# One broadcast product of 512 columns in the place of four of 128, its diagonals in one tile

## Chip, cores and metric

One Trainium2 chip (trn2), and one of its cores. The metric is the device time of one execution in microseconds (us). Times of instructions come from one profiled execution of the kernel.

## What is computed

A hybrid encoder layer runs over a prompt of 512 tokens and a sample of 1024 tokens with the same weights (width 1024, f32). It is RMSNorm, one combined input projection, differential attention with four heads beside a gated linear recurrence (RG-LRU), one output projection, RMSNorm, a SwiGLU feed-forward part and a last RMSNorm:

```python
def rmsnorm(x, g):
    xf = x.astype(jnp.float32)
    y = xf * lax.rsqrt(jnp.mean(xf * xf, axis=-1, keepdims=True) + NORM_EPS)
    return (y * g.astype(jnp.float32)).astype(x.dtype)
...
    h = rmsnorm(x, norm_mix)
    proj = h @ w_in
...
    o = diff_attention(q, k, v, lam)
    o = rmsnorm(o, subln_g) * (1.0 - lam_init)
...
    x = x + jnp.concatenate([o.astype(x.dtype), y_lru], axis=-1) @ w_out
    h2 = rmsnorm(x, norm_ffn)
    x = x + (jax.nn.silu(h2 @ w_gate) * (h2 @ w_up)) @ w_down
```

The change concerns the step that turns 1/rms, one number for each token, into a tile that can be multiplied with activations. It serves the norms over the width and the norm of each attention head's output.

## The kernel before

**Layout.** Activations lie feature by token: 128 features on the partitions, 512 tokens (a block) along the free axis. Block 0 is the prompt, blocks 1 and 2 are the sample. Products in full precision are three products of rounded halves each (`mm3`, L213 to L215: activation high and weight high, activation low and weight high, activation high and weight low). A weight's halves are made by ScalarE (`wh`, L200) and VectorE (`wl`, L201), an activation's by L326 and L327.

**Spreading 1/rms.** In this layout a token's sum of squares is a sum over partitions. `inv_rms_cols` (L274) makes it with one product for each 128 tokens, which leaves tokens on the partitions (`ss`, L279), and `rsqrt_cols` (L244) takes 1/sqrt by small VectorE steps (L248 to L253). `bcast_cols` (L256) brings the tokens back to the free axis and copies them to all partitions: it multiplies the identity by a column of 1/rms (`dg`, L261, a 128x128 diagonal matrix, VectorE), and a product with a matrix of ones (L262, TensorE) fills 128 columns of the PSUM bank `bc`. It does this for four groups of 128 tokens (two in the last stage). Each `dg` comes from the pool `small`, with 2 buffers of its own.

**Who calls it.** 22 calls: `load_block` (L297) once for each block, whose `bc` ScalarE copies to the row tile `rms` (L339); `attention` (L478), once for each prompt head and twice for each sample head, whose `bc` scales the head's output `ot` (L607, VectorE); the norm ahead of the feed-forward part; and the last norms (`finish`, L1086).

**The ring "mh".** Tiles of 128x512 f32 that live shortly are handed out by a ring, always in the order in which the program is written; a new one waits until the one that stood so many places before it is no longer used. In the first phase (input projections, recurrence, prompt attention) the ring has 4 buffers (L835), later it has 10 (`M3`, L902). In the first phase it serves the squares of `load_block` (`sqa`, `sq`), the evictions of the projection (`ev`, L375, VectorE multiplies a finished product by `rms`, and L376 stores it by DMA) and the reloads of `out_load` (`ir`, L617).

**Order of the work.** The program is written as generators that are interleaved by a table of shares (`advance`): the projection of the sample is the main stream in the first phase, and prompt attention, the recurrence and the prompt's output projection run as side streams between its products. The scheduler then sets the order on each engine; a row stays in that order on the chip. The projection (`proj`, L355) accumulates in 3 PSUM banks (`mm`, L834). Products of the projection are named `pm`, the gates of the recurrence `pr`, scores `sc`, their transposes `ptw` and `pt`, and the weighted values `pv`.

Of the kernel before, what the change touches and what calls it, by code (L numbers as in the profile page):

```python
# [16 lines left out]
ALU = mybir.AluOpType  # L17
# [3 lines left out]
P = 128  # L21
# [11 lines left out]
HALF = (P, BLK)  # L33
# [48 lines left out]
def build(tc, io, es):  # L82
    nc = tc.nc
    V, A, T = nc.vector, nc.scalar, nc.tensor
# [8 lines left out]
    rings = {}  # L93
# [7 lines left out]
    def small(n, name, bufs=2):  # L101
        return smp.tile([P, n], F32, name=name, tag=name, bufs=bufs)
# [8 lines left out]
    def bank(name, tag):  # L111
        return banks[tag].tile([P, BLK], F32, name=name, tag=tag)
# [13 lines left out]
    ident = cp.tile([P, P], F32, name="ident")  # L126
    nc.scalar.dma_start(ident, io["ident"])
    onesq = cp.tile([P, P], F32, name="onesq")
# [127 lines left out]
    def bcast_cols(tag, r, c0, who="m", n=4):  # L256

        bc = bank("bc", tag)
        for i in range(n):
            dg = small(P, "dg")  # L260
            V.tensor_scalar(dg, ident, r[:, c0 + i:c0 + i + 1], None, ALU.mult)  # L261
            T.matmul(bc[:, i * P:(i + 1) * P], lhsT=onesq, rhs=dg, start=True, stop=True)  # L262
        return bc[:, 0:n * P]

    def rms_rows(tag, x):
# [18 lines left out]
    def inv_rms(tag, acc, n=4):  # L284

        return bcast_cols(tag, inv_rms_cols(tag, acc, n), 0, n=n)
# [11 lines left out]
    def load_block(b, other=None, xring="raw"):  # L298
# [36 lines left out]
        if b:  # L335
            yield YL
        bc = bcast_cols("lru", r, 0)
        rows[b] = rings["rows"](HALF, f"rms{b}")
        A.copy(rows[b], bc)  # L339
# [143 lines left out]
    def attention(s, done, vo):  # L483
# [3 lines left out]
        for hd in range(NH):  # L487
# [116 lines left out]
            for g in range(n // BLK):  # L604
                w = slice(g * BLK, (g + 1) * BLK)
                bc = bcast_cols("pv", r, 4 * g, "a")
                V.scalar_tensor_tensor(ot[:, w], ot[:, w], subg, bc, ALU.mult, ALU.mult)  # L607
                nc.scalar.dma_start(cat[s][hd][:, w], ot[:, w])
                yield 1.5
# [217 lines left out]
    n = (B1 + B2 + 3 + GRP) // 2  # L827
# [49 lines left out]
    bc = inv_rms("pv", sums)  # L877
# [350 lines left out]
```

## Time and profile before

| what | value |
|---|---|
| median of 3 runs | 1773.88 us (1773.84 to 1776.88) |
| the profiled execution | 1773.56 us |
| its span in the trace | 1771.7 us |
| mean granted clock of TensorE, share of 2.4 GHz | 0.993 |
| TensorE busy | 1733.3 us (98%) |
| VectorE busy | 1316.5 us (74%) |
| ScalarE busy | 829.2 us (47%) |
| products of L262 | 168 passes, 26.8 us to 1764.6 us |

The profiled execution is 0.3 us under the median, and its span 1.9 us under its own time. PE is TensorE, DVE VectorE, ACT ScalarE. The busy time of a group of products counts each from its start to its modelled end, and products overlap: one of 512 columns has a length of about 0.4 us, but the next starts 0.23 us after it.

### The profile page before, as it was taken

What the parts mean: (1) busy time and instruction counts of PE and PEld (TensorE: products, weight loads), DVE (VectorE), ACT (ScalarE), POOL (GpSimd) and SP (SyncE); (2) the same over time, 40 slices, a digit from 0 to 9 for tenths busy, and PEclk for the clock granted to TensorE, in tenths of its full rate; (3) what the DMA queues carried; (4) which work ended last, traced back from release to release, by engine and by line L of the source; (5) the groups of instructions that cost most, each with busy time, mean ns of one, the idle gap of its engine ahead of it and who ended that gap; (6) DMA issues with size and microseconds to landing.
All of it is one profiled execution on the core that took longest, in us unless ns stands there. A gap on an engine that the chain in (4) does not pass through costs nothing.

```text
span 1771.7 us, 22720 instructions
## 1 busy us (share of the span) xinstructions
PE 1733.3 (98%) x8316; PEld 1432.2 (81%) x8316; DVE 1316.5 (74%) x2291; ACT 829.2 (47%) x1327; POOL 1.6 (0%) x6
## 2 busy tenths in 40 slices
PE   8999999999999999999999989999999999999997
PEld 7777787777878888888878768888888888888897
DVE  6789878777578777777453797777777777977784
ACT  6568556664355554545242452333233334445451
POOL 0000000000000000000000000000000000000000
PEclk9999999999999999999999999999999999999999
DMA  8533424153373322222364743222233229743261
GB/s 294 193 113 102 152 84 137 60 172 137 115 232 112 105 83 96 77 84 78 125 215 132 258 161 114 89 102 101 98 111 125 89 78 337 256 125 97 95 201 54
DMA packets 105023, 238.77 MB, mean 135 GB/s; under 512 B 12240, under 2 KB 21200, under 8 KB 104912
## 3 DMA queue, kind: packets, MB, share of 16 engines
q1 hardware_dynamic: 76608, 185.04, 32.8%
q10 hardware_dynamic: 28304, 52.28, 7.7%
q8 instruction: 65, 1.06, 0.2%
q14 instruction: 46, 0.38, 0.1%
HBM read 180.00 MB, written 57.28 MB: 134 GB/s over the span
## 4 chain that ended last, share of the span: by engine, by line
PE 84%; DVE 6%; DMA 4%; ACT 3%; issue 1%; SPq 0%; DVEq 0%; ACTq 0%
PE pm L213 5%; PE pm L214 5%; PE pm L215 4%; PE gu L213 4%; PE gu L215 4%; PE gu L214 4%; PE acc L215 4%; PE acc L213 4%; PE acc L214 4%; PE y L213 3%; PE y L214 3%; PE y L215 3%; PE z L214 2%; PE z L213 2%; PE z L215 2%; PE x L213 2%
## 5 line engine op out<-in xcount | busy, mean ns | idle before, releaser
L213 PE MATMUL pm<-xh,wh 128*128 128x512 f32 x480 | 190.5, 397 | 5.6 <-ACT wh L200 3.3
L214 PE MATMUL pm<-xl,wh 128*128 128x512 f32 x480 | 189.7, 395 | 0.8 <-DVE xl L327 0.8
L215 PE MATMUL pm<-xh,wl 128*128 128x512 f32 x480 | 189.4, 395 | 0.0
L200 ACT CAST wh<-wr 128x1024 fp32r<-128x1024 f32 x100 | 104.9, 1049 | 149.9 <-PE gu L214 61.3
L213 PE MATMUL gu<-yh,wh 128*128 128x512 f32 x352 | 142.0, 403 | 0.9 <-DVE ev L375 0.9
L213 PE MATMUL acc<-hp,ws 128*128 128x512 f32 (+1 forms) x396 | 140.9, 356 | 0.0
L215 PE MATMUL acc<-hp,ws 128*128 128x512 f32 (+1 forms) x396 | 140.5, 355 | 0.0
L214 PE MATMUL acc<-hp,ws 128*128 128x512 f32 (+1 forms) x396 | 140.2, 354 | 0.0
L215 PE MATMUL gu<-yh,wl 128*128 128x512 f32 x352 | 139.0, 395 | 0.0
L214 PE MATMUL gu<-yl,wh 128*128 128x512 f32 x352 | 138.7, 394 | 0.0
L201 DVE TENSOR_TENSOR wl<-wr,wh 128x1024 fp32r<-128x1024 f32 x100 | 122.0, 1220 | 17.8 <-ACT wh L200 16.9
L588 ACT ACTIVATE pb<-pb,mn 128x1024 f32<-128x1024 f32 (+1 forms) x96 | 96.9, 1009 | 73.0 <-DVE mn L585 72.9
L585 DVE CUSTOM_DVE_ANT_0 pb<-sc,tab 128x1024 f32<-128x1024 f32 (+1 forms) x96 | 100.0, 1041 | 33.3 <-PE sc L583 31.8
L703 ACT CAST ws<-s 128x512 fp32r<-128x512 f32 x88 | 54.6, 622 | 125.7 <-PE x L215 46.8
L213 PEld LDWEIGHTS pm<-xh,wh 128*128 128x128 f32 x480 | 90.9, 189 | 24.2 <-ACT wh L200 3.5
L214 PEld LDWEIGHTS pm<-xl,wh 128*128 128x128 f32 x480 | 90.8, 189 | 19.6 <-DVE xl L327 1.6
L215 PEld LDWEIGHTS pm<-xh,wl 128*128 128x128 f32 x480 | 90.6, 189 | 19.0 <-DVE wl L201 0.7
L141 ACT CAST hp<-hr 128x512 fp32r<-128x512 f32 (+1 forms) x143 | 77.2, 550 | 54.4 <-PE acc L215 24.6
L142 DVE TENSOR_TENSOR hp<-hr,hp 128x512 fp32r<-128x512 f32 (+1 forms) x143 | 84.6, 603 | 23.7 <-ACT hp L141 20.1
L703 ACT CAST ws<-wr 128x512 fp32r<-128x512 f32 x66 | 41.1, 622 | 100.8 <-PE z L215 43.8
L214 PEld LDWEIGHTS acc<-hp,ws 128*128 128x128 f32 x396 | 75.1, 190 | 10.4
L215 PEld LDWEIGHTS acc<-hp,ws 128*128 128x128 f32 x396 | 75.0, 189 | 10.4
(268 smaller groups left out, 4299.8 us busy)
## 6 DMA issues: line engine op xcount, KB each, us to landing
wr<-w_gate SPq DMA_DIRECT2D x44, 512.0 KB, 3.5
wr<-w_up SPq DMA_DIRECT2D x44, 512.0 KB, 3.5
wr<-w_in SPq DMA_DIRECT2D x40, 512.0 KB, 4.2
hr<-hs SPq DMA_DIRECT2D x77, 256.0 KB, 2.8
hs<-t ACTq DMA_DIRECT2D x44, 256.0 KB, 2.0
hs<-ht ACTq DMA_DIRECT2D x33, 256.0 KB, 2.8
wr<-w_out SPq DMA_DIRECT2D x16, 512.0 KB, 3.5
xd<-xh ACTq DMA_DIRECT2D x28, 256.0 KB, 2.1
```

The lines of the kernel that those rows point to most:

```text
L141: A.copy(h, src)
L142: eng.tensor_tensor(l, src, h.bitcast(F32), ALU.subtract)
L200: A.copy(h, r)
L201: V.tensor_tensor(l, r, h.bitcast(F32), ALU.subtract)
L213: T.matmul(out, lhsT=wh, rhs=ah, start=first, stop=False, skip_group_check=more)
L214: T.matmul(out, lhsT=wh, rhs=al, start=False, stop=False, skip_group_check=more)
L215: T.matmul(out, lhsT=wl, rhs=ah, start=False, stop=last, skip_group_check=more)
L585: V.tensor_tensor_reduce(out=pp[m], in0=sc, in1=tab[:, 896 - q0:896 - q0 + n], scale=-0.125, scalar=3e38, op0=ALU.add, op1=ALU.min, accum_ ...
L588: A.activation(pp[m], pp[m], AF.Exp, scale=-1.0, bias=mn, accum_out=zz)
L703: A.copy(h[:, 0], src)
```

## The change

A call takes one tile of 128x512 from the ring "mh". Four VectorE instructions write its quarters (two where n is 2), and one product of n x 128 columns follows.

```diff
     def bcast_cols(tag, r, c0, who="m", n=4):
 
         bc = bank("bc", tag)
+        dg = rings["mh"](HALF, "dg")
         for i in range(n):
-            dg = small(P, "dg")
-            V.tensor_scalar(dg, ident, r[:, c0 + i:c0 + i + 1], None, ALU.mult)
-            T.matmul(bc[:, i * P:(i + 1) * P], lhsT=onesq, rhs=dg, start=True, stop=True)
+            V.tensor_scalar(dg[:, i * P:(i + 1) * P], ident, r[:, c0 + i:c0 + i + 1], None, ALU.mult)
+        T.matmul(bc[:, 0:n * P], lhsT=onesq, rhs=dg[:, 0:n * P], start=True, stop=True)
         return bc[:, 0:n * P]
```

Three places show how the instructions move.

**VectorE, head 3 of the prompt's attention.** Names end in the number of their tile; numbers differ between the kernels. Before, the evictions of the projection (`ev`) that are written after this head's diagonals stand well ahead of them; the first piece is row 399 and its neighbours, the second begins at row 510.

```order
L366 MEMSET xrs_2977 128x1
L524 SCALAR_TENSOR_TENSOR cf_2299<-z04_2066,neglam_92,cf_2299 128x1
L375 TENSOR_TENSOR ev_2721<-pm_2696,rms1_1789 128x512
L525 SCALAR_TENSOR_TENSOR pb_2223<-pb_2223,cf_2299 128x512
...
L416 SCALAR_TENSOR_TENSOR xcv_3183<-xrs_2977,par_84,xcv_3183 128x1024
L261 TENSOR_SCALAR dg_2650<-ident_86,rsa4_2636 128x128
L261 TENSOR_SCALAR dg_2653<-ident_86,rsa4_2636 128x128
L365 MEMSET xrs_3148 128x2
L366 MEMSET xrs_3148 128x1
L372 TENSOR_TENSOR xrs_3148<-pm_3151,rms1_1789 128x512
L261 TENSOR_SCALAR dg_2656<-ident_86,rsa4_2636 128x128
```

Of the change, the rows from 466 on. There are no L375 and no L372 between row 399 (the scaling of head 2's output) and these diagonals.

```order
L252 SCALAR_TENSOR_TENSOR rta4_2601<-rta4_2601,ov4_2389 128x4
L253 SCALAR_TENSOR_TENSOR rsa4_2600<-rta4_2601,rsa4_2600 128x4
L261 TENSOR_SCALAR dg_2614<-ident_86,rsa4_2600 128x128 x4
L375 TENSOR_TENSOR ev_2679<-pm_2654,rms1_1771 128x512
L375 TENSOR_TENSOR ev_2722<-pm_2697,rms2_1957 128x512
L607 SCALAR_TENSOR_TENSOR ot_2387<-ot_2387,subg_93,bc_2613 128x512
L375 TENSOR_TENSOR ev_2788<-pm_2763,rms1_1771 128x512
L375 TENSOR_TENSOR ev_2832<-pm_2807,rms2_1957 128x512
L201 TENSOR_TENSOR wl_2862<-wr_2859,wh_2861 128x1024
L375 TENSOR_TENSOR ev_2890<-pm_2865,rms1_1771 128x512
```

Six evictions (`ev_2721` to `ev_2968` before) moved from ahead of the diagonals to behind them, the first of them by 69 rows.

**TensorE, the products of that head.** Before, products of the projection (`pm`) stand among the gates and the head's products; this is where the head's transposes of v begin.

```order
L213 MATMUL pr_2877<-xch_2735,gh_2726 128x512
L214 MATMUL pr_2877<-xcl_2736,gh_2726 128x512
L215 MATMUL pr_2877<-xch_2735,gl_2727 128x512
L213 MATMUL pm_2907<-xh11_559,wh_2692 128x512
L214 MATMUL pm_2907<-xl11_563,wh_2692 128x512
L514 MATMUL pt_2416<-ident_86,vr_2413 128x128 x4
L215 MATMUL pm_2907<-xh11_559,wl_2693 128x512
L213 MATMUL pm_2907<-xh12_560,wh_2692 128x512
```

Of the change, the rows from 1003 on, and from 1061 on; no row between them is a product of the projection.

```order
L215 MATMUL pm_2763<-xh13_555,wl_2530 128x512
L213 MATMUL pr_2797<-xch_2693,gh_2684 128x512
...
L514 MATMUL pt_2380<-ident_86,vr_2377 128x128 x4
L213 MATMUL pr_2835<-xch_2693,gh_2684 128x512
L582 MATMUL sc2_2402<-kt_2372,qh_2395 128x512
L583 MATMUL sc2_2402<-kt_2372,ql_2396 128x512
...
L215 MATMUL pv_2580<-wth0_2560,v_2379 128x256
L556 MATMUL pv_2580<-onesq_88,osq_2594 128x1 x2
L262 MATMUL bc_2613<-dg_2614,onesq_88 128x512
L213 MATMUL pm_2807<-xh20_1773,wh_2529 128x512
```

Between the broadcast of head 2 and that of head 3 stood 209 products of the projection before and stand 26 now, the last of them at row 1003; of the gates there are 18 and 24, and the head's own products are the same.

**ScalarE, block 1.** After the copy of the row tile (`rms`, L339) comes the third weight of the projection (`wh`, L200). Before:

```order
L339 COPY rms_1789<-bc 128x512
L307 ACTIVATE sq<-xc 128x512
L200 CAST wh<-wr 128x1024
L455 ACT_TABLE_LOAD
L455 ACTIVATE tr<-tr 128x1024
L376 DMA qkvs_109<-ev 128x512
L326 ACTIVATE xh_1793<-xc,par 128x512
```

Of the change:

```order
L339 COPY rms_1771<-bc 128x512
L307 ACTIVATE sq<-xc 128x512
L326 ACTIVATE xh_1775<-xc,par 128x512
L455 ACT_TABLE_LOAD
L455 ACTIVATE tr<-tr 128x1024
L307 ACTIVATE sq<-xc 128x512
L200 CAST wh<-wr 128x1024
```

The weight moved behind one L326, a table load, one L455 and one more square.

## Rows read from the trace of the kernel before

**Rows 1.** The profile's page: busy us by engine, share of the span.

```profile
PE 1733.3 (98%) x8316; PEld 1432.2 (81%) x8316; DVE 1316.5 (74%) x2291; ACT 829.2 (47%) x1327; POOL 1.6 (0%) x6
```

**Rows 2.** What TensorE waited for: us in total, times, longest us.

```profile
PE bc L262 <- DVE dg L261: 7.9, 7, 3.9
PE y L213 <- ACT ws L703: 5.5, 1, 5.5
```

**Rows 3.** Timeline of TensorE at head 2's broadcast: start us, length us, instruction.

```profile
252.53 0.68 PE L262 MATMUL bc<-dg,onesq 128*128 128x128 f32 x4
252.96 0.47 PE L213 MATMUL pr<-xch,gh 128*128 128x512 f32 x1
253.37 0.71 PE L262 MATMUL bc<-dg,onesq 128*128 128x128 f32 x4
```

**Rows 4.** Timeline of VectorE from head 2's diagonals to head 3's.

```profile
252.09 0.48 DVE L261 TENSOR_SCALAR dg<-ident,rsa 128x128 f32<-128x128 f32 x2
253.02 0.51 DVE L261 TENSOR_SCALAR dg<-ident,rsa 128x128 f32<-128x128 f32 x2 [0.45 <-PE bc L262]
...
257.15 1.22 DVE L447 SCALAR_TENSOR_TENSOR ti<-ti,xcv 128x1024 f32<-128x1024 f32 x1 [2.29 <-ACT ti L440]
...
317.05 0.47 DVE L261 TENSOR_SCALAR dg<-ident,rsa 128x128 f32<-128x128 f32 x2
```

**Rows 5.** Windows around the stretch between these broadcasts: us, busy us by engine, clock.

```profile
252.50:317.50 65.00, 64.32 (x305) 51.48 (x304) 52.86 (x100) 42.20 (x65) 0.00 (x0) 1.00 0.40 129
317.50:410.00 92.50, 91.81 (x401) 73.08 (x400) 68.81 (x91) 62.62 (x73) 0.00 (x0) 1.00 0.41 138
```

**Rows 6.** VectorE's groups by shape, 257 to 317.5 us: busy us, mean ns.

```profile
L201 DVE TENSOR_TENSOR wl<-wr,wh 128x1024 fp32r<-128x1024 f32 x4 | 4.8, 1212 | 0.0
L142 DVE TENSOR_TENSOR il<-ir,ih 128x512 fp32r<-128x512 f32 x7 | 4.8, 684 | 3.4 <-ACT ih L141 3.4
L416 DVE SCALAR_TENSOR_TENSOR xcv<-xrs,par,xcv 128x1024 f32<-128x1024 f32 x3 | 3.8, 1277 | 0.0
L375 DVE TENSOR_TENSOR ev<-pm,rms 128x512 f32<-128x512 f32 x4 | 2.7, 678 | 0.7 <-PE pm L215 0.7
L372 DVE TENSOR_TENSOR xrs<-pm,rms 128x512 f32<-128x512 f32 x3 | 2.0, 683 | 0.0
```

**Rows 7.** Timeline of TensorE, 292 to 295 us, among head 3's products.

```profile
292.69 0.40 PE L582 MATMUL sc<-kt,qh 128*128 128x512 f32 x1
292.92 0.39 PE L583 MATMUL sc<-kt,ql 128*128 128x512 f32 x1
...
294.46 0.28 PE L214 MATMUL pv<-wtl,v 128*128 128x256 f32 x1
294.58 0.28 PE L215 MATMUL pv<-wth,v 128*128 128x256 f32 x1
```

**Rows 8.** Timeline of ScalarE and TensorE at block 1's broadcast.

```profile
172.01 0.56 ACT L339 COPY rms<-bc 128x512 f32<-128x512 f32 x1
...
173.00 1.04 ACT L200 CAST wh<-wr 128x1024 fp32r<-128x1024 f32 x1
174.06 1.28 ACT L455 ACT_TABLE_LOAD   x1
...
174.09 0.79 PE L213 MATMUL pm<-xh,wh 128*128 128x512 f32 x1 [3.27 <-ACT wh L200]
...
175.35 1.06 ACT L455 ACTIVATE tr<-tr 128x1024 f32<-128x1024 f32 x1
...
176.31 0.71 ACT L326 ACTIVATE xh<-xc,par 128x512 fp32r<-128x512 f32 x1
176.93 0.61 ACT L307 ACTIVATE sq<-xc 128x512 f32<-128x512 f32 x1
```

**Rows 9.** Windows behind two of TensorE's gaps: us, busy us, clock.

```profile
172.40:179.10 6.70, 5.01 (x11) 3.58 (x12) 6.54 (x11) 6.34 (x9) 0.00 (x0) 0.50 0.34 117
...
1059.80:1066.60 6.80, 5.78 (x14) 4.54 (x15) 5.56 (x10) 3.53 (x7) 0.00 (x0) 0.50 0.34 113
```

## The prediction

> **What bounds the kernel now.** The page comes first: TensorE is busy for 1733.3 of 1771.7 us, VectorE for 74% and ScalarE for 47% [rows 1]. So 38.4 us are all that TensorE loses, and whatever makes it idle for longer, with no idle time later to win back, is paid in full. The second view is what TensorE waits for: the broadcast's own wait for its diagonals is the largest entry, and small (7.9 us in 7 waits, 3.9 of them in one) [rows 2]. The third is the timeline of one broadcast in a busy stretch: two diagonals, a pair of them multiplied, then a product of another stream, then the other pair, 252.53 to 253.37 us [rows 3]. VectorE makes the third diagonal only after the first product has freed one of the two buffers, and sits for 0.45 us for it [rows 4]. That is the wait that the change removes. The fourth is a table of windows: from 252.5 to 317.5 us TensorE is busy for 64.32 of 65 us, because products of the projection fill every wait of attention and recurrence; VectorE is busy for 52.86 us there [rows 5]. This filling is what the prediction is about.
>
> **The product itself.** A pair is four passes (two for each diagonal, 128 columns each), and what follows it starts 0.43 us later: 0.11 us for a pass [rows 3]. A call is eight of these, 0.86 us. Now it is two passes of 512 columns. No row shows a pass of 512 columns of this kind; by its columns, four times 0.11, it is 0.43 us and the call 0.86 us, an estimate from these rows. I cost the exchange at nothing. The Trainium skill says in "Perfetto Trace Analysis", section Optimizing Tensor Performance, that larger matmuls are more efficient than smaller ones. By it the sum would be some tenths of a us lower per call; the rows, where passes of 128 columns already follow each other at the pace of their columns, show nothing to be won there.
>
> **The diagonals.** The same 84 VectorE instructions remain. The wait between pairs goes: it is 0.45 us of VectorE and on TensorE the rest of 0.41 us that one product of 0.23 us does not fill [rows 3, 4], about 0.2 us for each of 20 calls. In return the product waits for the fourth diagonal instead of the first. Three more at 0.25 us are 0.75 us, which TensorE has other products for in most places. I take -2 us, from -3.5 (all pair gaps gone) to +3.5 (the later start is exposed in most calls).
>
> **The ring.** The diagonals now stand in line in "mh". With 4 buffers in the first phase, an eviction of the projection that is written later than a head's diagonals can get its buffer only after them. The order shows that this binds once, at head 3 of the prompt: between the broadcasts of heads 2 and 3 there is neither an `ev` nor a gate or recurrence eviction on VectorE. The 3 banks of the projection fill up, and TensorE has 26 products of the projection there in place of 209. TensorE then runs at the pace of head 3's own chain (scores, VectorE's minimum, ScalarE's exponential, transposes, values). Its length, from the start of one broadcast to the start of the next:
> - To the first instruction of the recurrence that leads the stretch (L447): before, 257.15 - 252.53 = 4.6 us [rows 3, 4], with 10 products between the broadcast and the last gate product that it needs. Now 30 stand there, 20 more at 0.23 us (spacing of products of 512 columns [rows 7]) = 4.6, so 9.2 us.
> - From L447 to the diagonals of head 3: 317.05 - 257.15 = 59.9 us before [rows 4]. What leaves VectorE in between is 4 `ev`, 4 `xrs` and `gt` evictions and 7 `il` at 0.6 us from start to start (durations of 0.68), 4 `wl` at 1.14 and 3 L416 at 1.2 (durations 1.21 and 1.28) [rows 6]: 9.0 + 4.6 + 3.6 = 17.2 us. VectorE carries this stretch, so I take 59.9 - 17.2 = 42.7 us.
> - From the first diagonal to the product: 0.44 us before [rows 3, 4], with three more diagonals at 0.25 us 1.2 us.
>
> That is 53.1 us. TensorE's work in it is 26 products of the projection, 24 gates and 16 scores, 66 at 0.23 = 15.2 us; 24 value products of 256 columns at 0.12 [rows 7] = 2.9; 20 transposes and the broadcast's 8 passes at 0.11 [rows 3] = 3.1; small sums 0.3. Together 21.5 us. TensorE idles for **53.1 - 21.5 = 31.6 us**. The projection's products that were put off (183 at 0.23 us, 42 us) run afterwards in stretches where TensorE is busy already (91.81 of 92.5 us [rows 5]), so nothing comes back.
>
> The low end is VectorE without any wait: 52.86 - 17.2 = 35.7 us, with the longer start of the product 36.5, so 15 us of idle time. The high end is 31.6 us and a chain made longer by a slow clock (below).
>
> No row of the trace before shows an eviction waiting for a buffer of the ring; by rows alone this term would be 0. The Trainium skill, "Perfetto Trace Analysis", section Identifying Performance Opportunities, says that a gap repeating for a stretch on the engine that should be saturated can mean that there isn't enough SBUF or PSUM for the next tile. By it the sum has the 31.6 us, and without it -2 us are left. I go with the order on the engines, in which the projection is absent from that stretch.
>
> **The third weight of block 1.** TensorE waits for 3.27 us at 174.09 until ScalarE has made `wh`, 173.00 to 174.04 [rows 8]. Now `wh` stands behind L326 (0.62 from start to start), the table load 1.28, L455 0.96 and a square 0.51 [rows 8]: 3.4 us, and the last gate products ahead of the broadcast stand later by about 1 us. `wl` follows on VectorE. I take +5 us. It can be 0 if products on hand cover it, and 6 with the half clock that followed this gap (below).
>
> **The clock.** The granted clock was 0.50 (1.2 GHz) in the windows behind a gap of 3.27 us and one of 5.50 us [rows 2, 8, 9], with TensorE busy before each. At 0.50 there are 11 and 14 products and groups in 6.7 to 6.8 us, where the row tells of idle time too. After the long stretch, TensorE resumes at half clock, for up to the 6.8 us of these windows, which costs up to half of that, 0 to 3.4 us: I take +2.5 us. If the clock stays at half within the stretch, the head's value products, transposes and scores on the chain (2.9 + 2.2 + 3.7 us) double: up to +8.8 us.
>
> **Elsewhere** broadcasts stand exposed at the start (26.8 us), at the norms of the feed-forward part and at the end; there the four diagonals and one product take as long as two pairs with their gap, within 0.3 us each. I cost them at 0: the later start of the product is paid by the shorter way behind it. Where another work covers this, a lost cover costs 0.75 us. In the later phases the ring has 10 buffers, and in the order no such stretch appears.
>
> **Sum.** 31.6 + 5 - 2 + 2.5 = +37.1 us on the profiled execution's 1773.56 us: **1811 us** (1773.56 is 0.3 us under the median, which this cannot tell apart). About 0.2%, 3.5 us, is what a measurement of this kernel can tell from no change.
>
> **Rivals.**
> - *A milder stretch.* VectorE keeps going, because ScalarE is always ahead: 15 us in place of 31.6, with 3 for the weight and 1 for the clock: +17, 1791 us. For it speaks that VectorE had only 12 us without work in 65 [rows 5]. Against it: those waits were filled with evictions that are now gone, and every step of the head passes through three engines.
> - *A heavier stretch.* TensorE stays at 1.2 GHz in it, and the head's chain grows by up to 8.8 us, with 6 for the weight and the pair term at its upper end: 31.6 + 8.8 + 6 + 3.4 + 3.5 = +53, 1827 us. For it: TensorE would be busy for 40% of the stretch, and half clock followed both gaps [rows 9].
> - *Not slower.* VectorE and ScalarE run ahead of TensorE when it comes to head 2's broadcast, far enough to have the recurrence's part of the stretch done, so that TensorE finds its operands ready and only pair gaps vanish: -3.5 us, 1770 us. This decides from a lead of some 32 us. Against it: head 2's first diagonal starts 0.44 us before its product [rows 3, 4], so VectorE has no lead there, and the ring itself holds the lead down. The Trainium skill's sentence on larger matmuls points this way too.
>
> **Chances.** My forecast, 1800 to 1820 us: 0.68. Milder: 0.13. Heavier: 0.14. Not slower: 0.05, most of it faster by over 0.2%. The range of 8 in 10 takes in the two rivals' values: **1791 to 1827 us**. Faster by over 0.2%: 0.03; within 0.2%: 0.02; slower: 0.95.
>
> **What would show it.** Right: in the new profile TensorE's busy time is about the same, its idle time larger by some 35 us, nearly all of it in one stretch of about 53 us between the broadcasts of heads 2 and 3 of the prompt, with few `pm` products there, VectorE nearly busy through it, and the waits of TensorE put down to head 3's steps (VectorE's `mn`, ScalarE's casts and `xch`). Two passes of 0.43 us for a broadcast. A gap of about 8 us for `wh` in block 1. Wrong: products of the projection running between those broadcasts, or that stretch under 40 us long, or the waits spread over all heads. If the stretch is as forecast and the time is not, then the cover at the other broadcasts was misjudged.

## The result, and the profile after

The changed kernel takes 1812.47 us (median of 4 runs, 1812.21 to 1814.68), the kernel before 1773.86 us (4 runs): a ratio of 1.0222, 95% interval 1.0207 to 1.0237. That is 38.6 us more. The forecast was 1811 us. The profiled execution of the changed kernel took 1814.68 us (span 1812.9), 2.2 us over its median; against the profiled one of before that is +41.1 us, and readings from the two traces have to add up to that.

The first lines of the page after, the busy times and the granted clock of TensorE in 40 slices of the span (tenths of full speed):

```profile
PE 1743.6 (96%) x8192; PEld 1429.3 (79%) x8192; DVE 1320.7 (73%) x2291; ACT 829.4 (46%) x1327; POOL 1.6 (0%) x6
...
PEclk9998995999999999999999999999999999999998
```

VectorE and ScalarE do the same work as before [rows 1]. TensorE has 124 passes less (168 of the broadcast became 44) and is yet busy 10.3 us longer, and it sits idle for 69.3 us in place of 38.4. The clock row tells where to look: one slice at half speed, the seventh, which is 272 to 317 us.

What TensorE waits for now (us in total, times, longest us):

```profile
PE bc L262 <- DVE dg L261: 12.3, 10, 3.6
PE pm L213 <- ACT wh L200: 7.4, 1, 7.4
PE y L213 <- ACT ws L703: 6.0, 1, 6.0
PE ptw L534 <- DVE pb L525: 4.9, 2, 4.2
PE pv L556 <- ACT osq L551: 3.6, 2, 2.7
PE pr L213 <- ACT ti L440: 3.5, 1, 3.5
```

Beside [rows 2], the wait for `wh` has grown from 3.3 [rows 8] to 7.4 us, and waits have come that were not there: `ptw`, `pv`, `pr` are the products of a head and of the recurrence, all in one place. Windows of that place, from head 2's broadcast on (us, then busy us of PE, PEld, DVE, ACT, POOL with instructions, then clock, DMA share and GB/s):

```profile
252.80:263.00 10.20, 10.18 (x41) 7.64 (x42) 3.02 (x3) 5.97 (x8) 0.00 (x0) 1.00 0.41 130
263.00:312.30 49.30, 25.86 (x80) 16.95 (x78) 35.02 (x74) 28.97 (x48) 0.00 (x0) 0.58 0.13 43
312.30:322.00 9.70, 9.66 (x34) 7.24 (x35) 3.74 (x6) 1.06 (x1) 0.00 (x0) 0.83 0.29 110
```

In [rows 5] TensorE was busy for 64.32 of 65 us with 305 entries in this place; now 25.86 of 49.3 us with 80, and at a mean clock of 0.58. The projection's products between the two broadcasts are 26 (groups of TensorE by line, 252.8 to 312.3 us):

```profile
L214 PE MATMUL pm<-xl,wh 128*128 128x512 f32 x9 | 3.9, 438 | 0.0
...
L215 PE MATMUL pm<-xh,wl 128*128 128x512 f32 x9 | 3.5, 391 | 0.0
L213 PE MATMUL pm<-xh,wh 128*128 128x512 f32 x8 | 3.1, 391 | 0.0
```

VectorE's timeline through the stretch, which answers to [rows 4], and what VectorE waited for in it:

```profile
261.95 1.23 DVE L447 SCALAR_TENSOR_TENSOR ti<-ti,xcv 128x1024 f32<-128x1024 f32 x1 [5.45 <-ACT ti L440]
...
311.32 0.87 DVE L261 TENSOR_SCALAR dg<-ident,rsa 128x128 f32<-128x128 f32 x4
312.11 1.28 DVE L375 TENSOR_TENSOR ev<-pm,rms 128x512 f32<-128x512 f32 x2
```

```profile
DVE ti L447 <- ACT ti L440: 5.5, 1, 5.5
DVE pb L585 <- PE sc L583: 5.1, 6, 1.5
DVE ov L561 <- PE pv L556: 4.8, 1, 4.8
```

The two evictions start as soon as the four diagonals are written. Both ends of the stretch on TensorE:

```profile
252.82 1.10 PE L262 MATMUL bc<-dg,onesq 128*128 128x512 f32 x2 [0.23 <-DVE dg L261]
253.35 0.79 PE L214 MATMUL pm<-xl,wh 128*128 128x512 f32 x1
253.99 0.39 PE L215 MATMUL pm<-xh,wl 128*128 128x512 f32 x1
...
312.34 2.04 PE L262 MATMUL bc<-dg,onesq 128*128 128x512 f32 x2 [3.50 <-DVE dg L261]
313.39 1.42 PE L213 MATMUL pm<-xh,wh 128*128 128x512 f32 x1
...
315.46 0.45 PE L213 MATMUL pm<-xh,wh 128*128 128x512 f32 x1
315.75 0.40 PE L214 MATMUL pm<-xl,wh 128*128 128x512 f32 x1
```

From broadcast to broadcast it is 59.5 us; the forecast was 53.1. Block 1, to be read beside [rows 8] (timeline of ScalarE, and TensorE's next product):

```profile
171.60 0.57 ACT L339 COPY rms<-bc 128x512 f32<-128x512 f32 x1
...
172.60 0.71 ACT L326 ACTIVATE xh<-xc,par 128x512 fp32r<-128x512 f32 x1
173.33 1.28 ACT L455 ACT_TABLE_LOAD   x1
...
176.10 1.03 ACT L200 CAST wh<-wr 128x1024 fp32r<-128x1024 f32 x1
...
177.19 0.79 PE L213 MATMUL pm<-xh,wh 128*128 128x512 f32 x1 [7.43 <-ACT wh L200]
```

The weight's cast starts 4.5 us after the row tile's copy; before it was 1.0 us.

**Where the 41.1 us lie.** I set each product's spacing at full clock (0.227 us for 512 columns, 0.12 for 256, 0.108 for 128) against what elapsed, and add what TensorE lost by idle time and slow clock together. From 168.6 to 197.8 us it loses 12.6 us (before, in the same work, 7.2): +5.4. From head 2's broadcast to head 3's 37.8 (3.2): +34.6. From there to the prompt's next norm 5.1 (4.0): +1.1. In the last stage, 1712 us on, 10.4 (6.7): +3.7, of which 1.5 us are one wait for a `hp` at 1757 us. Behind it TensorE ran at half clock for some 3 us:

```profile
1759.50:1762.70 3.20, 3.20 (x17) 3.20 (x16) 1.77 (x5) 1.24 (x4) 0.00 (x0) 0.50 0.84 260
```

The traces of the runs below show neither at this place; e2 and e3, with the diagonals in the ring too, lose 6.8 and 6.9 us in the last stage, and the profiled execution is 2.2 us over its median. So most of the +3.7 belongs to this one execution and not to the change. Everything else together is 3.7 us less than before, spread over the other stretches between broadcasts, none with more than 1.4 us.

### The profile page after: what moved, and what is told of

Same layout as the page of the kernel before. It is cut to its first block, busy times and chain, and to the rows that moved or that the text cites. A ratio compares the mean times of both kernels' runs of the same rounds, so it can differ in the third digit from the quotient of the medians.

```text
span 1812.9 us, 22498 instructions
## 1 busy us (share of the span) xinstructions
PE 1743.6 (96%) x8192; PEld 1429.3 (79%) x8192; DVE 1320.7 (73%) x2291; ACT 829.4 (46%) x1327; POOL 1.6 (0%) x6
## 4 chain that ended last, share of the span: by engine, by line
PE 74%; DVE 4%; DMA 2%; issue 1%; ACT 1%; DVEq 0%; SPq 0%; ACTq 0%
PE gu L215 4%; PE gu L213 4%; PE gu L214 4%; PE acc L215 3%; PE acc L214 3%; PE acc L213 3%; PE y L213 3%; PE y L214 3%; PE y L215 3%; PE pm L213 2%; PE pm L215 2%; PE pm L214 2%; PE z L213 2%; PE z L214 2%; PE z L215 2%; PE x L213 2%
## 5 line engine op out<-in xcount | busy, mean ns | idle before, releaser
L213 PE MATMUL pm<-xh,wh 128*128 128x512 f32 x480 | 191.4, 399 | 10.4 <-ACT wh L200 7.4
L200 ACT CAST wh<-wr 128x1024 fp32r<-128x1024 f32 x100 | 105.2, 1052 | 167.9 <-PE pm L214 73.0
```

The costliest lines, as they stand in the source:

```text
L200: A.copy(h, r)
L213: T.matmul(out, lhsT=wh, rhs=ah, start=first, stop=False, skip_group_check=more)
```

## Experiments

All runs stand against the kernel before, which was timed beside them (medians 1773.0, 1773.5 and 1772.4 us in the three groups e1 to e4, e5 to e8, e9 to e12). Each group ran on a chip of its own, so a difference between runs of two groups is uncertain by about 1 us more.

| run | diagonals in | product | ring | room made | us | ratio, 95% interval |
|---|---|---|---|---|---|---|
| the change | ring | 1 x 512 | 4 | no | 1812.5 | 1.0222 (1.0207 to 1.0237) |
| e1 | own tile | 1 x 512 | 4 | yes | 1779.9 | 1.0042 (1.0028 to 1.0056) |
| e2 | ring | 4 x 128 | 4 | no | 1815.7 | 1.0241 (1.0227 to 1.0255) |
| e3 | ring | 1 x 512 | 5 | yes | 1824.4 | 1.0291 (1.0276 to 1.0306) |
| e4 | own tile | 1 x 512 | 3 | no | 1769.1 | 0.9977 (0.9968 to 0.9986) |
| e5 | ring for heads, own for others | 1 x 512 | 4 | yes | 1819.1 | 1.0257 (1.0243 to 1.0271) |
| e6 | own for heads, ring for others | 1 x 512 | 4 | yes | 1788.1 | 1.0077 (1.0064 to 1.0091) |
| e7 | ring, extra products | 1 x 512 | 4 | no | 1811.9 | 1.0219 (1.0205 to 1.0233) |
| e8 | 4 small buffers | 4 x 128 | 4 | yes | 1781.9 | 1.0047 (1.0033 to 1.0060) |
| e9 | 2 small buffers, as before | 4 x 128 | 4 | yes | 1785.9 | 1.0080 (1.0067 to 1.0092) |
| e10 | 2 small buffers, as before | 4 x 128 | 3 | no | 1775.2 | 1.0012 (1.0004 to 1.0021) |
| e11 | own for heads, ring for others | 1 x 512 | 3 | no | 1776.9 | 1.0024 (1.0014 to 1.0034) |
| e12 | 4 small buffers | 4 x 128 | 3 | no | 1768.0 | 0.9973 (0.9964 to 0.9982) |

"Room made" is this edit, since the SBUF has no room for a tile more beside the others in the first phase:

```diff
-    pool(es, "edge_left").tile([P, 32], F32, name="edge_left")
+    pool(es, "edge_left").tile([P, 8], F32, name="edge_left")
-    es.enter_context(tc.tile_pool(name="edge", bufs=1, side="right")).tile([P, 56], F32, name="edge")
+    es.enter_context(tc.tile_pool(name="edge", bufs=1, side="right")).tile([P, 8], F32, name="edge")
-                    xr = rings["xr"]([P, SEQ_S + 32], f"xr{s}")
+                    xr = rings["xr"]([P, SEQ_S + 4], f"xr{s}")
```

(The padding shrinks by 288 bytes and the conv tile by 112; the expectation of the first run counts the padding whole.) I took it to be free. It is not, so runs with it are compared with one another, and runs without it likewise.

**What room costs (e9).** The kernel before with that edit alone.

> The kernel before, its order unchanged, with only the room made as in the runs with a tile of its own and with five buffers: 352 bytes per partition of padding and 28 unused columns of the conv tile left out. Theory (other addresses of the tiles make products in the stages after 1000 us start 228 to 232 ns apart in place of 227, as in the runs that made room so): 1780 to 1787 us. Rival (the excess of those runs came from the diagonals' tile): 1772 to 1775 us.

It took 1785.9 us, 13.4 over the kernel before, and the rows of TensorE, VectorE and ScalarE stand in exactly the order of before. Windows of the stage after 1200 us, of e9 and of before:

```profile
1200.00:1300.00 100.00, 100.00 (x435) 81.41 (x434) 74.47 (x116) 29.23 (x51) 0.00 (x0) 1.00 0.31 109
```

```profile
1200.00:1300.00 100.00, 100.00 (x443) 82.85 (x442) 74.81 (x116) 29.80 (x51) 0.00 (x0) 1.00 0.31 108
```

Both are full at full clock, and e9 gets through 8 products less in 100 us. Its groups say the same (from 1100 to 1600 us, two groups, first of e9, then of before):

```profile
L213 PE MATMUL acc<-hp,ws 128*128 128x512 f32 x120 | 47.2, 393 | 0.0
...
L213 PE MATMUL y<-b5512h,ws 128*128 128x512 f32 x80 | 31.7, 396 | 0.0
```

```profile
L213 PE MATMUL acc<-hp,ws 128*128 128x512 f32 x132 | 51.4, 389 | 0.0
L213 PE MATMUL y<-b5512h,ws 128*128 128x512 f32 x80 | 31.1, 389 | 0.0
```

The edit changes the sizes of three tiles and so the addresses of others; in that stage no other difference is known. No broadcast runs between 1018 and 1674 us of the kernel before, and this stage, from one broadcast to the next, takes 664.3 us in e9 and 656.1 us before. Its length will be of use below, since what a run wins or loses in it does not come from a broadcast.

**The tile in the ring, or the product (e1, e2).**

```diff
-        dg = rings["mh"](HALF, "dg")
+        dg = small(BLK, "dg", 1)
```

> The one product of 512 columns stays, its tile comes from a buffer of its own and not from the ring. Theory (the ring's line is the loss): the projection runs again between the broadcasts of heads 2 and 3, no gap of 7 us for the third weight; 1768 to 1775 us, at or a little under the kernel before. Rival (one product behind four diagonals is itself the loss): the time stays near 1812 us, with the waits for dg spread over the calls. To make room, 352 bytes per partition of padding and 28 unused columns of the conv tile are left out.

1779.9 us, outside what either theory said, because of the room. Against e9 it is -5.9 us; its trace has no stretch (TensorE's loss from head 2's broadcast to head 3's is 3.3 us by the sum above; the window between them):

```profile
252.00:316.80 64.80, 63.95 (x297) 50.34 (x297) 53.09 (x99) 43.03 (x65) 0.00 (x0) 1.00 0.39 127
```

So one product behind four diagonals is not the loss.

```diff
-        T.matmul(bc[:, 0:n * P], lhsT=onesq, rhs=dg[:, 0:n * P], start=True, stop=True)
+        for i in range(n):
+            w = slice(i * P, (i + 1) * P)
+            T.matmul(bc[:, w], lhsT=onesq, rhs=dg[:, w], start=True, stop=True)
```

> The diagonals lie in the ring's tile as in the change, but four products of 128 columns spread them as before. Theory (ring): the stretch without the projection is there in full, about 59 us between the broadcasts of heads 2 and 3, 1810 to 1816 us. Rival (the product's shape): 1772 to 1776 us.

1815.7 us, and the stretch is there, 59.2 us (window between the broadcasts):

```profile
255.50:314.70 59.20, 37.83 (x130) 26.06 (x130) 37.91 (x77) 34.95 (x55) 0.00 (x0) 0.64 0.18 58
```

The ring's tile alone brings the loss, with the old products.

**The place in the line, or too few buffers (e3, e4, e10).**

```diff
-    ring(left, "mh", 4)
+    ring(left, "mh", 5)
```

> The change, with 5 buffers in the ring in the first phase in place of 4 (room made as in the run with its own tile). Theory A (a tile of the ring is handed out only after those written before it, however many are free): the stretch stays, 1810 to 1815 us. Rival B (too few buffers): evictions get the fifth buffer, the stretch shrinks by some 10 us or more, under 1803 us.

1824.4 us, above what I gave, again by the room: against e9 it is +38.6 us, what the change costs against the kernel before. The order has the same 26 products of the projection in the stretch (in the traces TensorE and ScalarE run the order of the change throughout, and on VectorE one `il` stands elsewhere), and the stretch is about as long, 58.7 us (its part behind the last of them):

```profile
262.00:310.50 48.50, 25.54 (x80) 16.04 (x79) 35.07 (x74) 28.97 (x48) 0.00 (x0) 0.64 0.13 43
```

A fifth buffer changes nothing in the stretch. The reverse, an own tile and a ring of 3:

> The diagonals have a tile of their own, and the ring has only 3 buffers in the first phase. Theory A (the place in the line): no stretch, 1768 to 1777 us even with fewer buffers. Rival B (too few buffers): evictions wait more than in the change or as much, over 1800 us.

1769.1 us. TensorE is full again from head 2's broadcast to head 3's:

```profile
253.70:319.20 65.50, 65.14 (x303) 51.30 (x302) 54.26 (x100) 43.81 (x66) 0.00 (x0) 1.00 0.38 126
```

Fewer buffers, no stretch. Rival B falls in both runs; that the diagonals stand in the ring's line decides, and whether the ring has 3, 4 or 5 buffers does not (more were not tried). It is 0.23% under the kernel before, interval 0.14 to 0.32%: it beats both. The control, the kernel before with a ring of 3:

> The kernel before with 3 buffers in the ring in the first phase, diagonals as before. Control for the run with three buffers and one product: if the gain of that run comes from the diagonals, this one stays at 1772 to 1775 us; if it comes from the smaller ring, it falls to 1767 to 1771 us. A ring too small would give more than 1776 us.

1775.2 us: the smaller ring, with the addresses that come with it, costs 2.7 us, so the gain of e4, 6.1 us against this control, is the diagonals'. The stage without broadcasts takes 653.6 us in e4 and 653.2 us in e10, so the gain does not lie there.

**Two losses (e5, e6, e11).** A call knows whether it serves a head (`who` is "a"):

```diff
-        dg = rings["mh"](HALF, "dg")
+        dg = rings["mh"](HALF, "dg") if who == "a" else small(BLK, "dg", 1)
```

> The heads' broadcasts take their tile from the ring, all others (row tiles of the blocks, norms) one of their own; one product of 512 columns each. Theory (two separate losses): the stretch at head 3 stays (about 59 us, TensorE idle or at half clock for some 38 us of it), the wait for the third weight of block 1 is back at 3 to 5 us: 1806 to 1811 us. Rival (the weight's wait comes from the heads' tiles as well): 1811 to 1815 us.

1819.1 us, above both ranges, again by the room; against e1, which has the same room, +39.2 us. The stretch is 57.8 us, and the wait for the third weight is back at 3.3 us:

```profile
251.00:308.80 57.80, 32.87 (x112) 20.79 (x112) 38.01 (x76) 33.85 (x53) 0.00 (x0) 0.68 0.19 59
```

```profile
PE pm L213 <- ACT wh L200: 3.3, 1, 3.3
```

The reverse (the heads' tile of their own, the others' in the ring):

> The reverse: the heads' broadcasts have a tile of their own, all others take one of the ring. Theory: no stretch at head 3, but the third weight of block 1 stays late on ScalarE, with a gap of 7 us or more: 1775 to 1781 us. Rival (no loss without the heads' tiles in the ring): 1769 to 1774 us.

1788.1 us, above both ranges too, and +8.1 against e1; no stretch, but the weight's wait is there:

```profile
PE pm L213 <- ACT wh L200: 6.7, 1, 6.7
```

The same without the room, with a ring of 3:

> One product of 512 columns everywhere; the heads' broadcasts have a tile of their own, all others take one of the ring of 3; tile addresses as in the run with three buffers and all diagonals in a tile of their own (1769 us), from which it differs in the tile of the blocks' and norms' broadcasts alone. Theory (the third weight of block 1 is late by itself): 5 to 10 us above that run, 1774 to 1780 us, with a gap of about 7 us for that weight. Rival: within 2 us of that run.

1776.9 us, +7.8 against e4. So the two losses are separate: 39 us from the heads' tile, 8 us from that of the blocks and norms. With the gain of e1 (-5.9 us against e9) they come to 41 us, beside the 38.6 us of the change.

**The half clock (e7).** 48 extra products in the stretch (each two passes), tied to data of the head:

```diff
+                for _ in range(k if warm else 0):
+                    T.matmul(live[0][:, 384:512], lhsT=ident, rhs=src[:, 0:P], start=True, stop=True)
...
+                fill(vr, 16)
...
+                    fill(pp[m], 4)
```

> The change, with 48 extra products of 128 columns at head 3 of the prompt (about 10 us of TensorE work at full clock), which start when v or a tile of weights is ready and whose results are not used. Theory (the half clock made the head's chain longer): the granted clock in the stretch is near 1 for a good part, and the stretch is 2 to 6 us shorter than in the change in spite of the work: 1806 to 1811 us. Rival (the chain waits for VectorE and ScalarE, the clock does not matter): same length or longer by 1 to 5 us, 1812 to 1818 us.

1811.9 us, no difference from the change that can be told. The stretch is 2.3 us longer (61.8 us), though TensorE's mean granted clock in it was 0.84 in place of the change's 0.65, and for 10 us of its second half it was the full one:

```profile
298.00:303.00 5.00, 3.96 (x27) 3.09 (x26) 3.73 (x10) 2.50 (x8) 0.00 (x0) 0.99 0.26 105
303.00:308.00 5.00, 3.73 (x29) 3.21 (x28) 2.15 (x4) 1.13 (x3) 0.00 (x0) 1.00 0.00 0
```

The theory's 2 to 6 us did not show, and the stretch is as the rival said, same or longer by 1 to 5 us. It is no clean test, though: VectorE's waits for the scores and the values' sums did fall (from 5.1 and 4.8 to 3.1 and 3.3 us), but the extra products also moved other instructions of the three engines against each other, among them an operand of the head for which VectorE now waited 3.8 us. What part of the stretch the half clock makes stays open.

**What the pair wait is worth (e8, e12).**

```diff
-            dg = small(P, "dg")
+            dg = small(P, "dg", 4)
```

> The kernel before with 4 small buffers for the diagonals in place of 2, four products of 128 columns each. No diagonal waits for a product any more, so the wait inside the pairs goes and nothing else: 1768 to 1774 us. If the pair waits were covered anyway: 1773 to 1775 us, no change.

1781.9 us, above both ranges by the room, and against e9 -3.9 us. Of these, 1.7 us lie in the stage without broadcasts (662.6 us in place of 664.3) and are not the diagonals'. Without the room, ring of 3:

> Four small diagonals with 4 buffers and four products of 128 columns, 3 buffers in the ring. If the gain of the run with one product comes from the end of the wait inside the pairs, this one gains as much: 1767 to 1771 us. If it comes from the single product of 512 columns: 1772 to 1775 us.

1768.0 us: 0.27% under the kernel before (0.18 to 0.36%), 7.1 us under its control e10, and 1.1 us from e4; its stage without broadcasts takes 653.1 us, as in e10. VectorE's wait for a freed diagonal (who waited for the diagonals, us and times; before, then e12):

```profile
  DVE dg L261: 6.7, 16
```

```profile
  DVE dg L261: 0.2, 1
```

The edit gives the diagonals two buffers more, the wait ends and the time falls; how much of the gain is the wait itself and how much the order of other instructions, which moved with it, is not told apart. Whether one product or four spread the result makes no difference that e4 and e12 can tell.

## Why the prediction was right

**The ring's line at head 3** was the loss. Forecast 31.6 us idle and 2.5 us of slow clock behind it, 34.1; the trace has +34.6 in the stretch and +1.1 after it, and e5 against e1 +39.2 us. The reason in the text is half of it. "With 4 buffers ... can get its buffer only after them" was right about the line and left open whether the number mattered: e3 and e4 show that it does not. The rule of the Trainium skill that was weighed ("Perfetto Trace Analysis", section Identifying Performance Opportunities: a gap repeating on the engine that should be saturated can mean there isn't enough SBUF or PSUM for the next tile, buffer count or tile sizes) fits the gap, but a lack of buffers, which it gives as what may stand behind it, is not what the runs show here: the stretch is 58.7 us with 5 buffers in place of 59.5.

**The stretch's length by parts.** To L447 9.1 us (forecast 9.2). From the first diagonal to the product 1.02 (1.2). From L447 to the diagonals 49.4 us (42.7): this term was mis-sized. "VectorE carries this stretch" was its step; VectorE is busy for 38 of 59.5 us, and it waits for TensorE for 5.1 us at the scores and 4.8 us at the values' sums. Before, these waits were 0.5 and 0.7 us (257 to 317.5 us):

```profile
DVE ov L561 <- PE pv L556: 0.7, 2, 0.4
...
DVE pb L585 <- PE sc L583: 0.5, 2, 0.3
```

So VectorE's work did not carry the stretch alone: with 14.8 us of it gone (38.0 in place of 52.9 us busy) the part from L447 on became 10.5 us shorter and not 17.2. That the evictions of before filled waits of the head's chain through three engines, which now lie bare, is the likely reading. TensorE itself was at 1.2 GHz for most of it (mean 0.58 from 263 to 312.3 us), which the forecast had only as its heavier rival; how much of the 6.7 us this makes is not shown (e7). For the same reasons two of the forecast's signs failed: VectorE is not nearly busy in the stretch, and TensorE's busy time is not the same. It is 10.3 us more and the idle time 30.9 us more, because TensorE was busy for 36.0 us of the 59.5 with work that takes some 21.7 at full clock.

**That the sum, +37.1 us, came out so near the measured 38.6 is in part luck.** The stretch was 6.4 us longer than forecast (59.5 for 53.1). Against this stand 3.2 us that TensorE lost in this place before and that the forecast did not take off, 1.4 us less behind the stretch (1.1 for 2.5) and 1.7 us more won elsewhere (3.7 for 2). These nearly cancel.

**The third weight of block 1**: forecast +5, trace +5.4, runs e6 and e11 +8.1 and +7.8 where the tile of the blocks' and norms' diagonals is the one difference. The mechanism, ScalarE's cast behind L326, the table load, L455 and a square, stands in the rows as the order had it. e11's other order of ScalarE puts one more square and one more L326 in front of it, so its figure isn't the change's own.

**The pair waits**: forecast -2, bounds -3.5 and +3.5. The remainder of the trace is -3.7, and the comparisons at the same room and ring are -5.9 (e1 to e9), -3.9 (e8 to e9), -6.1 (e4 to e10) and -7.1 us (e12 to e10); of the first two, 1.2 and 1.7 us lie in the stage without broadcasts (663.1, 662.6 and 664.3 us in e1, e8 and e9). The gain was under-sized: counted was TensorE's unfilled gap alone. That VectorE, 6.7 us earlier free over 16 places, is then ahead for what comes next would explain the rest; this is argued, not shown.

**The product**: 0.86 us a call was forecast from the pace of columns. At head 2 the next product starts 0.53 us after the broadcast's first pass, but its own successor only 0.64 us later in place of 0.23: 0.94 us together. That the exchange brings and costs nothing is also what e4 and e12 say, 1.1 us apart. The Trainium skill's sentence on larger matmuls ("Perfetto Trace Analysis", section Optimizing Tensor Performance) points to a gain per call that no run here shows.

**Not slower** fell: VectorE had no lead at head 2, and it waits 5.45 us for ScalarE at L447. **The last stage**, costed at 0, is 0 but for the one wait and the half clock behind it in the profiled execution.

## What to carry to other kernels

A tile that is taken from a shared ring joins a line: what is written after it cannot pass it, and here a fifth buffer did not help. Before a short-lived tile is moved into such a ring, look in the order on the engines for what used to run ahead of it; a helper on a slow side chain belongs in a tile of its own, if need be by one buffer taken from the ring. And when two small buffers make an engine wait, two more of them are worth trying before the products are changed: here, with the ring of 3, they give as much as the single product (7.1 and 6.1 us).

## What was not expected of the hardware

Shifting tiles by a few hundred bytes per partition changed the pace of TensorE: 435 in place of 443 products in 100 us at full clock, with mean lengths of 393 and 396 in place of 389 ns in the two groups shown, 13.4 us over the whole kernel at the same order (e9). Which of the three trimmed tiles does it, and what property of an address decides, was not tried.

The clock in the stretch (windows of the changed kernel, as above):

```profile
265.00:268.00 3.00, 1.50 (x7) 0.93 (x7) 1.82 (x3) 1.77 (x3) 0.00 (x0) 0.97 0.29 87
268.00:271.00 3.00, 0.31 (x2) 0.00 (x0) 1.68 (x2) 2.97 (x4) 0.00 (x0) 0.50 0.32 96
292.00:295.00 3.00, 0.90 (x6) 0.42 (x4) 2.96 (x7) 2.97 (x4) 0.00 (x0) 1.00 0.00 0
```

TensorE fell to 1.2 GHz at about 268 us, after a gap of 2.1 and one of 0.7 us and ahead of the one of 3.5, where the two gaps that the forecast looked at were 3.3 and 5.5 us [rows 2, 8, 9]. Single shorter gaps were followed by half clock as well: the 1.5 us at 1757 us above, and in e9 a gap of 1.4 us ahead of 30.2 us, with half clock from 31.1 us. In the stretch it stayed there for some 44 of the 48 us that followed, apart from a few around 293, and was back at 2.4 GHz at about 315.5 us, some 3 us after the broadcast had ended the stretch; the forecast allowed up to 6.8 us.
